# A two-layer hybrid step on one core: the first modulation, the first norm and the filter network in another order

## Chip, cores and metric

One core of one Trainium2 chip runs the whole program. The metric is the device time of one execution in microseconds (us); of several runs the median counts. The engines are TensorE (PE in the rows; PEld is its weight load), VectorE (DVE), ScalarE (ACT), GpSimd (POOL) and SyncE (SP, which issues the loads).

## The reference

Two layers process 128 context tokens and 256 latent tokens of width 1024 with the same weights, each group with its own condition vector. Of each layer the change touches the opening only:

```
mod = silu(cond) @ w_mod + b_mod
sh1, sc1, g1, sh2, sc2, g2 = split(mod, 6)
h = rms_norm(x, norm1) * (1 + sc1) + sh1
proj = h @ w_in
kf = hyena_filters(L, w1, b1, w2, b2, w3, freq)
```

`proj` feeds grouped-query attention, multi-head latent attention and a Hyena long convolution, whose spectra `kf` come out of a small filter network (two sine layers, taps with a window, an L1 norm, a Fourier transform) that does not depend on x. Branches, output projection and a ConvFFN follow.

## The kernel before

The 384 tokens stand side by side as columns, channels on the partitions: x is `xa`, 8 tiles of 128 x 384. Matmuls against weights are made of three products of a high and a low part (`mm3`, L269 to L271); `hi_lo` makes the parts (a ScalarE copy, L231, and a VectorE subtraction, L235) for weights that `load_w` (L249) brings in pieces of 1 MB through a ring of two buffers.

The first stage has four strands:

- **Modulation vectors** (`mod_load`, `mod_vec`): a vector of 1024 numbers for both conditions takes four loads of 1 MB (L329) and matmuls of 32 x 512 outputs (L338; one load is 4 instructions, 8 rows of the trace). ScalarE copies the result (L231), TensorE transposes it (L302), and VectorE adds it up with the bias (L238, 128x16) and, for vector 1, forms the scale factors `avs` (L241, 128x16). Vectors 0 and 1, shift and scale, are wanted by the first norm. Their eight loads go to `early` buffers that nothing else uses yet.
- **Squares and first norm** (`squares`, `norm_h`): ScalarE squares the x tiles (L310), VectorE sums them; TensorE adds over partitions (L382), ScalarE takes the root (L364), and TensorE spreads `rstd` over a bank (L388). Then, for each of 8 tiles, VectorE multiplies x by it (L238), ScalarE modulates the two token groups (L396, 128 and 256 columns), and the parts are made: even tiles on VectorE (cast L403, subtraction), odd ones by `hi_lo`.
- **Filter network** (`filters`): two sine layers (L428 to L436, with L460 and L464), then four jobs, for two channel halves and two orders. A job prepares weights (`prep`), makes three groups of taps (`taps`, L503, drained by a VectorE multiplication, L238; for two of them GpSimd forms a mean, L510), sums their sizes (`sizes`, L521; L538), and transforms them (`spectra`: ScalarE builds a diagonal, L546 spreads it, L558 are the transforms in three groups, each drained by VectorE, and GpSimd adds a bias at the end, L566). The filter network is a generator; each `next` issues one step.
- **First projection** (`hyena_in`): six tiles of 24 matmuls (L269 to L271) that need h and split weights.

`weave(main, (side, rate))` issues `rate` steps of a side strand for each step of `main`. Issue order is only the default: a scheduler orders each engine's instructions by priority, which follows the issue order, and by when it holds their inputs to be ready. `urgent(line, by)` issues every step of a strand at a priority raised by `by` places:

```
with tc.high_priority(offset=by):
    if next(line, line) is line:
        return
```

Within an engine the order so made is fixed, and an instruction that waits holds up all that stand behind it.

The PSUM banks are dealt out in turn, in issue order. In the first stage the filters turn through banks 0 to 3, norm and transposes through 4 to 6, modulation has 7. Once the first projection is issued (`PS_HY0`), its tiles turn through banks 1, 2 and 3, and the filters through 0 and 5. A tile that gets a bank waits until its last user is drained.

SP issues loads in its own order, with at most eight outstanding: each waits for the one eight places ahead of it.

Of the kernel before, what the change touches and what calls it, by code (L numbers as in the profile page):

```python
# [10 lines left out]
AF = mybir.ActivationFunctionType  # L11
# [30 lines left out]
SLABS = (1408, *[3072] * 9)  # L42
N_EXTRA = 3584
R_RE = 0.25
R_F0 = 3
U_CH, U_MLA = 20, 20
U_AV = 2000
FILL = (3, 2, 3)
# [137 lines left out]
def kernel(  # L186
# [8 lines left out]
    act, dve, pool, pe, sp = nc.scalar, nc.vector, nc.gpsimd, nc.tensor, nc.sync  # L195
# [83 lines left out]
    ident = ident_b.ap()  # L279
# [5 lines left out]
    cT = base.alloc(KD, 32).ap()  # L285
# [19 lines left out]
    def add_sq(k, src, first):  # L305
        if first:
            sums.append(FA.alloc(T, top=True))
        acc = sums[0].ap()
        sq = temps.get().ap()
        act.activation(out=acc if first else sq, in_=src, func=AF.Square)  # L310
        if not first:
            tt(acc, acc, sq, ALU.add)

    def squares():
        for k in range(KD):
            add_sq(k, xa[:, k], k == 0)
            yield
# [8 lines left out]
    def mod_load(l, v, k, buf):  # L326
        raw = buf.ap(2, 1024)
        src = w_mod[l, k * 256:(k + 1) * 256, v * 1024:(v + 1) * 1024]
        sp.dma_start(out=raw, in_=src.rearrange("(k p) n -> p k n", p=128))  # L329
        return raw  # L330
# [284 lines left out]
    def hyena_start(l, spec):  # L615
        y = HyenaState()
        y.l, y.spec = l, spec
        y.tok, y.late = {}, []
        line = hyena_in(y, 0, h_parts)
        next(line)  # L620
        return y, line
# [696 lines left out]
    def urgent(line, by):  # L1318

        if by < 0:  # L1320
            yield from line
            return
        while True:
# [3 lines that stand above are left out]
            yield  # L1327

    def finish(*lines):
        for g in lines:  # L1330
            for _ in g:
                pass

    def weave(main, *sides):

        credit = [0.0] * len(sides)
        for _ in main:
            for i, (g, rate) in enumerate(sides):
                credit[i] += rate
                while credit[i] >= 1:  # L1340
                    credit[i] -= 1
                    next(g, None)

    def chain(*lines):
        for g in lines:
            yield from g
# [18 lines left out]
    early = [*raw_ring.bufs, *early_parts[0].cut(2048), *early_parts[1].cut(2048)]  # L1365
    spec = new_spec()
    fl = filters(0, RA, spec, True)
    next(fl)
    sp.dma_start(out=vecs[0], in_=p_vec[0])
    sp.dma_start(out=cT, in_=p_c)  # L1370
    next(fl)
    next(fl)
    next(fl)
    ready = [mod_load(0, 0, k, early[k]) for k in range(2)]
    sp.dma_start(out=ident, in_=t_ident)
    next(fl)
    for k in (2, 3):
        ready.append(mod_load(0, 0, k, early[k]))
    for k in (0, 4):
        sp.dma_start(out=xa[:, k:k + 4], in_=p_x[:, k:k + 4])  # L1380
    for k in range(4):
        ready.append(mod_load(0, 1, k, early[4 + k]))
    act.activation(out=cT[:, :, 0:2], in_=cT[:, :, 0:2], func=AF.Silu)
    weave(chain(mod_vec(0, 0, ready[:4]), mod_vec(0, 1, ready[4:])), (fl, R_F0), (squares(), 1.2))
    for b in early_parts:
        b.free()
    parts = split_slab.whole(F32R).cut(1024)
# [2 lines left out]
    h_parts += [b.ap(KD, T) for b in h_slab.whole(F32R).cut(KD * T)]  # L1390
    hT = h_parts
    y, main = hyena_start(0, spec)
    finish(norm_h(0, 0))
    for i in range(2):
        rt = t_rope[i * 128:(i + 1) * 128]
        sp.dma_start(out=rope_a[:, i], in_=rt[:, 0:128].rearrange("p (a b) -> p a b", a=2))
# [2 lines left out]
    for l in range(NL):  # L1399
# [52 lines left out]
        if l + 1 < NL:  # L1452
            spec = new_spec()
            fl = filters(l + 1, RA, spec)
# [148 lines left out]
```

## Time and profile before

| | us |
|---|---|
| median of 3 runs | 1503.31 (1502.71 to 1505.6) |
| the profiled execution | 1507.35 |
| its span in the profile | 1505.2 |
| TensorE busy | 1460.2 (97%) |
| VectorE busy | 1005.3 (67%) |
| ScalarE busy | 750.7 (50%) |
| GpSimd busy | 97.1 (6%) |

The profiled execution is one of its own: its time is 4.0 us over the median of the runs, and its span lies 2.15 us within its time. Starts in the rows count from the beginning of the span. A row gives start, duration, engine, line, what is written and read, the count of instructions merged in it, and in brackets the idle time of the engine ahead of it with what ended that. The granted clock (PEclk) is 1.00 at 2.4 GHz and 0.50 at 1.2 GHz.

### The profile page before, as it was taken

The page shows a single profiled execution, that of the slowest core. Times are in us where ns is not written, and L with a number is a line of the kernel's source. Part 1 is how long each engine was busy: PE and PEld are TensorE (multiplying, and loading weights), DVE is VectorE, ACT ScalarE, POOL GpSimd, SP SyncE. Part 2 cuts the span into 40 slices and gives each one's busy share as a digit, 9 for nine tenths or more (in the row PEclk, how much of TensorE's full clock was granted, in tenths as well). Part 3 has the DMA queues.
Part 4 walks back from the last instruction along what each step waited for, and adds up shares of the span by engine and source line. Part 5 has one row for each costly group of instructions (what it writes and reads, how often), then busy time and mean ns, then how long its engine had stood idle before and what let it go on. Part 6 is the DMA issues. An engine that isn't in the chain of part 4 may idle for free.

```text
span 1505.2 us, 22120 instructions
## 1 busy us (share of the span) xinstructions
PE 1460.2 (97%) x8574; PEld 1342.2 (89%) x8574; DVE 1005.3 (67%) x1920; ACT 750.7 (50%) x1376; POOL 97.1 (6%) x125
## 2 busy tenths in 40 slices
PE   5799999999999999999999999999999999999997
PEld 3589889989889899999997888999888989999997
DVE  5758569547447886686775766884655777567674
ACT  4644456455444663454545444855555464344343
POOL 0222210000000000000000212100000000000000
PEclk9899999999999999999999999999999999999999
DMA  9444354434466542343266345332333533433431
GB/s 366 146 134 157 135 164 140 114 105 126 140 211 233 191 134 95 125 126 128 85 226 220 124 142 180 103 102 88 90 122 114 184 110 113 139 102 122 156 116 52
DMA packets 177496, 212.84 MB, mean 141 GB/s; under 512 B 24176, under 2 KB 160112, under 8 KB 177392
## 3 DMA queue, kind: packets, MB, share of 16 engines
q1 hardware_dynamic: 176528, 206.99, 42.6%
q0 software_dynamic: 864, 4.46, 0.9%
q8 instruction: 67, 1.10, 0.3%
q14 instruction: 37, 0.30, 0.1%
HBM read 209.29 MB, written 2.13 MB: 140 GB/s over the span
## 4 chain that ended last, share of the span: by engine, by line
PE 92%; DVE 3%; ACT 2%; DMA 1%; issue 1%; SPq 0%; DVEq 0%; ACTq 0%
PE banks L269 27%; PE banks L270 26%; PE banks L271 26%; PE banks L302 3%; PE banks L338 3%; PE banks L922 3%; DVE s L238 2%; PE banks L954 2%; PE banks L558 1%; DMA base<-in_w_in_dram 1%; DVE split L235 1%; PE banks L503 1%; ACT s L231 1%; PE banks L538 0%; DMA s<-in_p_w_dram 0%
## 5 line engine op out<-in xcount | busy, mean ns | idle before, releaser
L231 ACT ACTIVATE split<-base 128x1024 fp32r<-128x1024 f32 (+2 forms) x272 | 280.8, 1040 | 374.1 <-PE banks L270 264.1
L235 DVE TENSOR_TENSOR split<-base,split 128x1024 fp32r<-128x1024 f32 (+2 forms) x272 | 332.0, 1225 | 181.4 <-ACT split L231 180.8
L269 PE MATMUL banks<-h,split 128*128 128x384 f32 x1280 | 432.9, 342 | 5.2 <-DVE h L403 3.6
L270 PE MATMUL banks<-h,split 128*128 128x384 f32 x1280 | 435.9, 341 | 0.3
L271 PE MATMUL banks<-h,split 128*128 128x384 f32 x1280 | 433.2, 339 | 0.0
L269 PEld LDWEIGHTS banks<-h,split 128*128 128x128 f32 x1280 | 241.4, 189 | 19.5 <-issue 8.4
L270 PEld LDWEIGHTS banks<-h,split 128*128 128x128 f32 x1280 | 242.1, 189 | 4.6 <-issue 1.6
L271 PEld LDWEIGHTS banks<-h,split 128*128 128x128 f32 x1280 | 241.6, 189 | 2.4 <-issue 0.7
L270 PE MATMUL banks<-s,split 128*128 128x384 f32 x672 | 225.8, 337 | 0.0
L271 PE MATMUL banks<-s,split 128*128 128x384 f32 x672 | 225.6, 338 | 0.0
L269 PE MATMUL banks<-s,split 128*128 128x384 f32 x672 | 223.2, 339 | 1.0 <-ACT s L231 0.8
L241 DVE SCALAR_TENSOR_TENSOR s<-banks,base,s 128x127 f32<-128x127 f32 (+1 forms) x448 | 172.6, 411 | 8.4 <-ACT s L417 4.3
L231 ACT ACTIVATE s<-banks 128x384 f32<-128x384 f32 (+11 forms) x212 | 94.4, 472 | 101.3 <-PE banks L271 38.7
L231 ACT ACTIVATE s<-s 128x384 fp32r<-128x384 f32 (+3 forms) x142 | 79.0, 562 | 103.9 <-DVE s L238 57.6
L269 PEld LDWEIGHTS banks<-s,split 128*128 128x128 f32 x672 | 125.6, 188 | 4.4 <-ACT s L231 1.4
L271 PEld LDWEIGHTS banks<-s,split 128*128 128x128 f32 x672 | 126.1, 188 | 2.0 <-DVE base L241 0.8
L270 PEld LDWEIGHTS banks<-s,split 128*128 128x128 f32 x672 | 126.2, 188 | 1.4 <-issue 0.2
L238 DVE TENSOR_TENSOR s<-banks,s 128x512 f32<-128x512 f32 (+3 forms) x132 | 81.6, 645 | 43.7 <-PE banks L271 18.8
L241 DVE SCALAR_TENSOR_TENSOR base<-banks,base 128x128 f32<-128x128 f32 (+1 forms) x128 | 46.9, 412 | 74.8 <-PE banks L271 74.8
L238 DVE TENSOR_TENSOR s<-s 128x256 f32<-128x256 f32 (+4 forms) x122 | 68.0, 568 | 23.6 <-ACT s L1225 8.3
L302 PE MATMUL banks<-base,s 128*128 128x128 f32 x442 | 75.3, 274 | 2.3 <-DVE s L241 1.3
L417 ACT ACTIVATE s<-banks,base 128x384 f32<-128x384 f32 x112 | 73.2, 655 | 7.1 <-PE banks L271 7.1
(145 smaller groups left out, 1729.7 us busy)
## 6 DMA issues: line engine op xcount, KB each, us to landing
base<-in_w_in_dram SPq DMA_DIRECT2D x40, 1024.0 KB, 5.4
base<-in_ffn_up_dram SPq DMA_DIRECT2D x40, 1024.0 KB, 5.2
base<-in_w_mod_dram SPq DMA_DIRECT2D x28, 1024.0 KB, 5.2
s<-in_w_mod_dram SPq DMA_DIRECT2D x14, 1024.0 KB, 7.5
base<-in_ffn_down_dram SPq DMA_DIRECT2D x16, 896.0 KB, 5.0
base<-in_w_branch_dram SPq DMA_DIRECT2D x24, 512.0 KB, 3.5
base<-in_w_out_dram SPq DMA_DIRECT2D x8, 1024.0 KB, 5.4
base<-in_ffn_down_dram SPq DMA_DIRECT2D x8, 1024.0 KB, 5.3
```

Source lines behind the costliest of these rows:

```text
L231: act.activation(out=out, in_=in_, func=AF.Copy, scale=scale)
L235: dve.tensor_tensor(out=lo, in0=src, in1=f(hi), op=ALU.subtract)
L238: dve.tensor_tensor(out=out, in0=a, in1=b, op=op)
L241: dve.scalar_tensor_tensor(out=out, in0=a, scalar=s, in1=b, op0=op0, op1=op1)
L269: pe.matmul(out, l[0], r[0], start=start, stop=False)
L270: pe.matmul(out, l[0], r[1], start=False, stop=False)
L271: pe.matmul(out, l[1], r[0], start=False, stop=stop)
L302: pe.transpose(out, in_, ident[:n, :n])
L338: pe.matmul(gv[32 * j:32 * j + 32], cT[:, 2 * k + j // 2], raw[:, j // 2, (j % 2) * 512:(j % 2) * 512 + 512], start=k == 0, stop=k == KD / ...
L417: act.activation(out=dst, in_=src, func=AF.Identity, scale=vec(l, w1), bias=vec(l, bias))
L922: pe.matmul(out, q_of(h)[:, i * 128:(i + 1) * 128], k, start=m == 0, stop=m == len(ks) - 1)
L954: last = pe.matmul(p[b:b + 64, u], v, pT, start=start, stop=stop, tile_position=(0, b)).ins
```

## The change

The priority of five strands or parts of strands is raised by 3000 places (`U_M0`): the first three steps of the filter network (its two sine layers), both modulation vectors, the squares and the first norm. The first modulation load goes ahead of the filters' weights, the x loads and the identity are put among the modulation loads, and the second channel half's filter inputs behind the last of them. The activation of the condition vector is issued earlier. The weave issues 2.5 filter steps for each of its 12 modulation steps and not 3: 30 and not 36. No instruction is added or taken away.

```
-R_F0 = 3
+R_F0 = 2.5
+U_M0 = 3000
...
     fl = filters(0, RA, spec, True)
-    next(fl)
+    fl_now = urgent(fl, U_M0)
+    next(fl_now)
     sp.dma_start(out=vecs[0], in_=p_vec[0])
     sp.dma_start(out=cT, in_=p_c)
+    ready = [mod_load(0, 0, 0, early[0])]
+    act.activation(out=cT[:, :, 0:2], in_=cT[:, :, 0:2], func=AF.Silu)
+    next(fl_now)
+    next(fl_now)
     next(fl)
-    next(fl)
-    next(fl)
-    ready = [mod_load(0, 0, k, early[k]) for k in range(2)]
-    sp.dma_start(out=ident, in_=t_ident)
-    next(fl)
-    for k in (2, 3):
+    for k in (1, 2):
         ready.append(mod_load(0, 0, k, early[k]))
     for k in (0, 4):
         sp.dma_start(out=xa[:, k:k + 4], in_=p_x[:, k:k + 4])
+    ready.append(mod_load(0, 0, 3, early[3]))
+    sp.dma_start(out=ident, in_=t_ident)
     for k in range(4):
         ready.append(mod_load(0, 1, k, early[4 + k]))
-    act.activation(out=cT[:, :, 0:2], in_=cT[:, :, 0:2], func=AF.Silu)
-    weave(chain(mod_vec(0, 0, ready[:4]), mod_vec(0, 1, ready[4:])), (fl, R_F0), (squares(), 1.2))
+    next(fl)
+    weave(
+        urgent(chain(mod_vec(0, 0, ready[:4]), mod_vec(0, 1, ready[4:])), U_M0), (fl, R_F0), (urgent(squares(), U_M0), 1.2)
+    )
...
-    finish(norm_h(0, 0))
+    finish(urgent(norm_h(0, 0), U_M0))
```

What the scheduler makes of it is shown at three places. In the changed kernel every line from L45 on has a number that is higher by one, and by a few more behind the changed lines.

SP, the loads of the first stage from the fourth on, before (`p_w` is w3 and `p_win` the window, for one channel half each; `base`, `split` and `h` are the buffers of the modulation loads):

```order
L451 DMA s_1_138<-in_p_w_dram 128x1024
L453 DMA s_1_138<-in_p_win_dram 128x1280
L476 DMA s_1_141<-in_t_kdft_dram 128x1280
L329 DMA base_101<-in_w_mod_dram 128x2x1024 x2
L1375 DMA base_101<-in_t_ident_dram 128x128
L451 DMA s_1_141<-in_p_w_dram 128x1024
L453 DMA s_1_147<-in_p_win_dram 128x1280
L329 DMA split_108<-in_w_mod_dram 128x2x1024 x2
L1380 DMA base_101<-in_p_x_dram 128x1536 x2
L329 DMA split_108<-in_w_mod_dram 128x2x1024 x2
L329 DMA h_109<-in_w_mod_dram 128x2x1024 x2
```

and with the change:

```order
L330 DMA base_101<-in_w_mod_dram 128x2x1024
L452 DMA s_1_140<-in_p_w_dram 128x1024
L454 DMA s_1_140<-in_p_win_dram 128x1280
L477 DMA s_1_143<-in_t_kdft_dram 128x1280
L330 DMA base_101<-in_w_mod_dram 128x2x1024
L330 DMA split_108<-in_w_mod_dram 128x2x1024
L1381 DMA base_101<-in_p_x_dram 128x1536 x2
L330 DMA split_108<-in_w_mod_dram 128x2x1024
L1383 DMA base_101<-in_t_ident_dram 128x128
L330 DMA split_108<-in_w_mod_dram 128x2x1024 x2
L330 DMA h_109<-in_w_mod_dram 128x2x1024 x2
L452 DMA s_1_143<-in_p_w_dram 128x1024
```

The second w3 and window loads have moved from ahead of six modulation loads to behind the last, and x ahead of five of them.

TensorE, the last instructions ahead of the first projection matmul and that one, before:

```order
L338 MATMUL banks<-h_109,base_101 32x512 x4
L546 MATMUL banks<-s_1_141,base_101 128x512
L302 MATMUL banks<-base_101 128x128 x4
L388 MATMUL banks<-s_1_141,base_101 128x384
L503 MATMUL banks<-s_1_135 128x512 x6
L538 MATMUL banks<-base_101,s_1_211 128x1 x6
L558 MATMUL banks<-s_1_141 128x256
L558 MATMUL banks<-s_1_147,s_1_141 128x256
L558 MATMUL banks<-s_1_141 128x256
L558 MATMUL banks<-s_1_147,s_1_141 128x256
L269 MATMUL banks<-h_364,split_363 128x384 x3
```

and with the change:

```order
L339 MATMUL banks<-h_109,base_101 32x512 x8
L303 MATMUL banks<-base_101 128x128 x4
L547 MATMUL banks<-s_1_214,base_101 128x512
L559 MATMUL banks<-s_1_156,s_1_143 128x256
L559 MATMUL banks<-s_1_214,s_1_143 128x256
L559 MATMUL banks<-s_1_156,s_1_143 128x256
L559 MATMUL banks<-s_1_214,s_1_143 128x256
L504 MATMUL banks<-s_1_137 128x512 x6
L539 MATMUL banks<-base_101,s_1_156 128x1 x6
L270 MATMUL banks<-h_337,split_336 128x384
```

The norm's spread (L388, now L389) has gone ahead of the second vector's last loads, and less of the filters stands ahead of the projection. Instructions of the filters ahead of the first projection matmul, in TensorE's order as compiled:

| | taps L503 | spectra L558 | sums L538 | spreads L546 |
|---|---|---|---|---|
| before | 24 | 24 | 18 | 2 |
| with the change | 18 | 14 | 12 | 1 |

Further on, the first matmul of the attention's scores (L922) stands at place 1070 of TensorE's order before and 1133 with the change; the first that reads the attention's result stands at 1488 in both. From place 1860 on the two orders differ only in single neighbours.

VectorE, from the second vector's first addition (`base`, 128x16) to the first h tile's cast, before:

```order
L238 TENSOR_TENSOR base_101<-banks,base_101 128x16
L238 TENSOR_TENSOR s_1_107<-base_101,banks 128x384 x2
L235 TENSOR_TENSOR split_363<-base_101,split_363 128x1024
L238 TENSOR_TENSOR s_1_107<-base_101,banks 128x384 x2
L238 TENSOR_TENSOR s_1_141<-banks,s_1_147 128x512
L235 TENSOR_TENSOR split_363<-base_101,split_363 128x1024
L238 TENSOR_TENSOR s_1_211<-banks,s_1_147 128x512
L238 TENSOR_TENSOR base_101<-base_101,banks 128x16
L238 TENSOR_TENSOR s_1_147<-banks,s_1_147 128x512
L540 TENSOR_SCALAR s_1_147<-banks,base_101 128x4
L241 SCALAR_TENSOR_TENSOR base_101<-base_101 128x16
```

and with the change, from the third operation on a product of x and rstd behind the scale factors to the first drain of the third filter job's taps (ahead of these rows stand, behind the scale factors, the cast of the first h tile, two filter subtractions of 256 columns and the first h tile's low part):

```order
L239 TENSOR_TENSOR s_1_107<-base_101,banks 128x384
L404 CAST h_337<-s_1_107 128x384
L239 TENSOR_TENSOR s_1_107<-base_101,banks 128x384 x3
L239 TENSOR_TENSOR h_337<-s_1_107,h_337 128x384
L236 TENSOR_TENSOR split_336<-base_101,split_336 128x1024 x2
L239 TENSOR_TENSOR s_1_110<-banks,s_1_214 128x512 x3
L236 TENSOR_TENSOR h_337<-s_1_107,h_337 128x384
L239 TENSOR_TENSOR s_1_137<-s_1_214,s_1_137 64x512
L236 TENSOR_TENSOR h_337<-s_1_107,h_337 128x384
L236 TENSOR_TENSOR split_336<-base_101,split_336 128x1024 x2
L404 CAST h_337<-s_1_107 128x384
L239 TENSOR_TENSOR s_1_143<-banks,s_1_156 128x512
```

The vector's additions and factors now stand together with one subtraction between them, and the splits of the projection's weights, the drains of the first job's spectra and the first taps of the third job come behind them. GpSimd's addition of the first job (L566, now L567) is released by the third of the `x3` drains.

## Rows read from the trace of the kernel before

**Rows 1.** Windows: us, then PE, PEld, DVE, ACT, POOL busy, PEclk, DMA, GB/s.

```profile
300.00:400.00 100.00, 98.22 (x604) 86.72 (x603) 51.65 (x119) 51.84 (x105) 0.45 (x3) 1.00 0.42 121
```

**Rows 2.** Timeline of TensorE, 49 to 70 us.

```profile
49.75 1.06 PE L338 MATMUL banks<-h,base 128*32 128x512 f32 x8
...
52.24 0.66 PE L302 MATMUL banks<-base 128*128 128x128 f32 x4 [0.37 <-ACT base L231]
...
54.40 1.33 PE L503 MATMUL banks<-s 128*128 128x512 f32 x4 [0.36 <-DVE s L238]
55.59 1.50 PE L538 MATMUL banks<-base,s 128*128 128x1 f32 x12
62.64 1.22 PE L558 MATMUL banks<-s 128*128 128x256 f32 x2 [5.54 <-DVE s L540]
...
65.85 1.52 PE L269 MATMUL banks<-h,split 128*128 128x384 f32 x3
...
69.07 1.06 PE L338 MATMUL banks<-base 128*32 128x512 f32 x8
```

**Rows 3.** Windows of one us, columns as in rows 1.

```profile
58.00:59.00 1.00, 0.00 (x0) 0.00 (x0) 1.00 (x3) 0.00 (x0) 0.00 (x0) 0.79 0.41 131
...
68.00:69.00 1.00, 1.00 (x5) 0.79 (x3) 0.01 (x1) 1.00 (x3) 0.00 (x0) 0.59 0.00 0
69.00:70.00 1.00, 1.00 (x9) 0.16 (x8) 0.56 (x1) 1.00 (x4) 0.00 (x0) 1.00 0.06 16
```

**Rows 4.** Timeline of VectorE, 59 to 66 us.

```profile
59.96 1.21 DVE L235 TENSOR_TENSOR split<-base,split 128x1024 fp32r<-128x1024 f32 x1
61.09 0.68 DVE L238 TENSOR_TENSOR s<-banks,s 128x512 f32<-128x512 f32 x1
61.70 0.15 DVE L238 TENSOR_TENSOR base<-base,banks 128x16 f32<-128x16 f32 x1
...
62.50 0.16 DVE L241 SCALAR_TENSOR_TENSOR base<-base 128x16 f32<-128x16 f32 x1
...
64.50 0.36 DVE L403 CAST h<-s 128x384 fp32r<-128x384 f32 x1 [0.45 <-ACT s L396]
...
65.24 0.55 DVE L238 TENSOR_TENSOR h<-s,h 128x384 fp32r<-128x384 f32 x1
65.71 0.55 DVE L238 TENSOR_TENSOR s<-base,banks 128x384 f32<-128x384 f32 x1
```

**Rows 5.** Loads, 0 to 70 us: GB/s by 1.75 us; issues (KB, us to landing); SP's timeline.

```profile
GB/s 0 261 136 318 390 408 407 426 408 411 407 410 415 428 405 413 405 410 410 410 407 330 345 352 338 126 14 0 5 0 0 92 378 129 0 73 337 190 0 9
...
h<-in_w_mod_dram SPq DMA_DIRECT2D x2, 1024.0 KB, 18.6
...
18.22 3.96 SPq L329 DMA_DIRECT2D h<-in_w_mod_dram  x2
```

**Rows 6.** Timeline of ScalarE, 51 to 67 us.

```profile
51.62 0.57 ACT L231 ACTIVATE base<-banks 128x512 f32<-128x512 f32 x1
...
63.50 3.60 ACT L396 ACTIVATE s<-s,base 128x128 f32<-128x128 f32 x8
```

**Rows 7.** Timelines of GpSimd and VectorE, 55 to 59 us.

```profile
55.62 1.81 POOL L566 TENSOR_TENSOR s<-s,s 128x768 f32<-128x768 f32 x1 [9.05 <-DVE base L238]
...
56.47 2.04 DVE L235 TENSOR_TENSOR split<-base,split 128x1024 fp32r<-128x1024 f32 x1
```

**Rows 8.** Chain of waits, 67 to 103 us: start, us, what.

```profile
67.38 0.32 PE banks L270
...
84.71 1.23 PE banks L538 x12
...
98.51 0.18 PE banks L270
...
99.55 2.59 PE banks L558 x12
```

**Rows 9.** Line 922 (attention scores), to 420 us: ns min/median/max, first and last start.

```profile
L922 PE MATMUL banks<-s,s x92: 221/334/488, 245.5 to 415.7; 128*128 128x384 f32 x60, 128*128 128x128 f32 x32
```

## Prediction

> **What bounds the kernel now.** I read three views. The windows view comes first: in a stretch such as 300 to 400 us TensorE is busy 98.22 of 100 us and VectorE 51.65 [rows 1]. From about 70 us to the end the kernel is therefore a queue of TensorE work, and a change in the order of the first stage is worth what it takes out of TensorE's idle or slow time ahead of that queue, less nothing and plus nothing: work moved out of the idle time has to be done later.
>
> The timeline of TensorE shows that time [rows 2]. After the filter sums at 55.59 it stands idle for 5.54 us until 62.64, runs filter matmuls, and starts the first projection matmul at 65.85. In the windows of one us the granted clock falls inside 58 to 59 (0.79) and is back inside 68 to 69 (0.59), 1.00 at 69 [rows 3]; 0.50 is the 1.2 GHz level. So the 9 projection matmuls ahead of 69.07 (3 in the row of 65.85 and 6 behind it [rows 2]) ran at 0.32 us each and not at 0.18 [rows 8]. Had they run at the full clock, they would have had to start at 69.07 - 9 x 0.18 = 67.5. I call 67.5 the **effective start** of the queue.
>
> The timeline of VectorE shows why it starts so late [rows 4]. The last load of the second modulation vector is multiplied at 49.75 [rows 2], but VectorE adds it only at 61.70 and forms the norm's scale factors at 62.50; between, it splits weights and drains filter banks. The first h tile is cast at 64.50.
>
> **Part 1, the loads.** The last modulation load is issued from 18.22 on and takes 18.6 us [rows 5], so it lands at about 37.6. The queue moves some 410 GB/s at that time [rows 5], and serves loads in the order of issue. The new order takes one w3 and one window load (512 and 640 KB, 1.18 MB) from ahead of it: 2.9 us, so it lands at 34.7. The x loads come some 6 us earlier by the same count, and the first norm's squares, sums and square root with them; they finish near 33 and nothing waits for them, since the scale factors need the second vector. What SP now issues later (second filter half, rope tables) lands near 37, ahead of its users. The first projection weight lands near 40, before ScalarE is free for it at 42.3 below.
>
> **Part 2, the modulation vector.** From 34.7: 1.06 us of matmuls and 0.66 of transposes on TensorE [rows 2], 0.57 of copy on ScalarE [rows 6], together 37.0. VectorE then adds, does one filter subtraction that stands between the two adds and waits for a ScalarE copy queued behind the vector's own, and forms the factors: I put that at 38.5, against 62.66 before. This is what the change buys, 24 us on this value.
>
> **Part 3, from there to the first projection matmul.** ScalarE's eight modulating activations take 3.60 [rows 6]; the four narrow ones come first, so the first h tile is complete after about 2.2, at 40.8. From here VectorE is the only engine that matters, and works through the list shown with the change. The first projection tile needs bank 1. With 30 steps of the filter network issued instead of 36, that bank holds the first tap group of the third filter job, and its drain is the last row of that list. So I count to there: 8 operations of 384 columns at 0.47 (start to start), 3 casts at 0.36, 4 splits of 1024 columns at 1.13, 4 drains at 0.61 [rows 4], and three of other sizes for which I take 0.5, between the casts and the 384-column ones. That is 3.76 + 1.08 + 4.52 + 2.44 + 1.5 = 13.3 us.
>
> Into this list falls one GpSimd addition, which is released by the third drain. In the trace GpSimd ran it from 55.62 to 57.43, and the VectorE split that began at 56.47 took 2.04 and ended 1.08 after GpSimd did, where the same split alone takes 1.21 [rows 4, 7]. VectorE thus stood still until GpSimd was done. In the new list the operations behind the drain are splits and subtractions too, so I charge nearly the whole 1.81: 1.7 us. The Trainium skill (SBUF — State Buffer, Who interferes with whom) states the same for a VectorE instruction with two SBUF inputs: the second to come is blocked for the whole of the other. It speaks against this change, since it puts that piece on the critical list, and by it the charge is up to 1.8; by the loss of this one row alone (2.04 - 1.21) it would be 0.8.
>
> Sum: 40.8 + 13.3 + 1.7 = **55.8** for the first projection matmul, 10 us earlier than 65.85.
>
> **Part 4, the work that is left.** By the counts given with the change, 24 tap, 24 spectrum, 18 sum and 2 spread matmuls of the filters stood ahead of the first projection matmul, and now 18, 14, 12 and 1. What is pushed behind it costs full price in the queue: 6 taps at 0.33 [rows 2]; 10 spectrum matmuls of two passes, 20 x 0.216 = 4.3; 6 sums of two passes, 12 x 0.103 = 1.2 [rows 8]; the spread matmul has twice the columns of a spectrum pass, 0.86. Together 2.0 + 4.3 + 1.2 + 0.9 = **8.4 us** (7.7 if a tap falls to the cost of its 512 columns, about 0.23). The other moved matmuls (modulation, transposes, norm) stand ahead of it in both.
>
> **Part 5, the clock at the new start.** At the full clock the gain is 67.5 - 55.8 - 8.4 = **3.3 us**. But TensorE has pauses here too. After the spread matmul (done at 39) it waits until VectorE has taken the last product with rstd out of bank 5, which I put at 44.6; then it has some 8 us of filter work at the low level, and pauses again for about 3 us before 55.8. In the old trace the level fell 1.7 us into a pause of 5.5 and came back 6.2 us after work resumed [rows 2, 3]. If the same happens here, about 6.2 us of the queue run at half speed, 3.1 us are lost, and the gain is **0.2**. Both ends stand; I take 1.5, nearer to the low one, because the pause is longer than the 1.7 us after which the level fell. The Trainium skill (TensorE: Matmul & The Clock Gate, Part 1) says that the number of slow matmuls after a pause varies from run to run of one kernel; no row here shows that.
>
> The profiled execution took 1507.35 us, span 1505.2, and lies 4.0 over the median of 1503.31. The parts above are differences within it, and I carry the difference to the median: 1503.3 - 1.5 = **1501.8 us**. A measurement of this kernel can tell about 0.2% or 3 us from no change, so this forecast is "same".
>
> **The rivals.**
>
> *Faster, chance 0.34.* TensorE is at the full clock at the new start, and VectorE reaches the drain without the GpSimd collision: 3.3 + 1.7 = 5.0, 1498.3 us. For it: ScalarE and the loads have slack ahead of VectorE all along the list, and TensorE has more work shortly ahead of the start (8 us) than before. Against it: the list is VectorE's alone, and every wait in it adds. It counts as faster from a gain of 3.0.
>
> *Slower, chance 0.13.* The filter work that is pushed behind the start delays the Hyena chain and what follows it. By the places given with the change, the first score matmul of the attention now stands at 1133 and not 1070, while the matmuls that read the attention's result (first at 1488) have not moved; 63 places at about 0.18 are 11 us less time for the softmax. Before, those matmuls ran from 245.5 on [rows 9], and 1.78 us of 300 to 400 were idle [rows 1]. If its slack is 5 us and not 11, TensorE waits 6 us there, and 1501.8 + 6 gives 1508 us. It decides from 4.5 us of new waiting on. Against it: VectorE and ScalarE are each about half busy in that stretch (51.65 and 51.84 of 100).
>
> *No effect, within the forecast.* The raised steps could merely displace others, with VectorE equally late. The order speaks against it: fewer VectorE operations stand ahead of the first h tile.
>
> **How the numbers follow.** Forecast (within 0.2%, 1500.3 to 1506.3): 0.53. Faster 0.34, slower 0.13. The range goes from the faster rival with another 1.3 us for an earlier VectorE (1497.0) to 1505.0, which leaves out most of the slower rival. The forecast's own part of it is 1500.0 (full clock) to 1503.1 (6.2 us low), and a us or two more for VectorE's list.
>
> **What would show it.** Right: last modulation load near 34.7; scale factors near 38.5; first projection matmul near 56, released by VectorE's drain of a filter bank; granted clock 0.5 for some us from there; spectrum matmuls among the projections until about 120 us; no new TensorE waits at 240 to 340. Wrong: a start before 53 or after 59, a clock of 1.00 through the start, or TensorE idle after 70 us where it was not.

## Result and profile after

The changed kernel takes **1517.76 us** (median of 4 runs, 1515.96 to 1518.83) against 1504.05 (1502.71 to 1505.6) of the kernel before, measured beside it: ratio 1.0084, 95% interval 1.0072 to 1.0097. It is 13 us slower; the forecast was 1501.8 and its range ended at 1505.0. The profiled execution took 1517.78 us, with a span 10.7 us longer than before's 1505.2. (The profiled execution of before, 1507.35, lies 3.3 us over this median, so the two traces show 10.7 of the 13.7 us.) The page, first lines and the row of the projections (busy, mean ns, idle time ahead and what ended it):

```profile
span 1515.9 us, 22111 instructions
...
PE 1466.9 (97%) x8574; PEld 1346.7 (89%) x8574; DVE 1005.4 (66%) x1920; ACT 752.3 (50%) x1376; POOL 97.4 (6%) x125
...
L270 PE MATMUL banks<-h,split 128*128 128x384 f32 x1280 | 433.8, 342 | 11.1 <-DVE s L239 5.4
```

All of it has come about by 463 us. ScalarE's first square of the second norm, before and then changed, comes 10.6 us later, and from there to the end the distance stays about that (10.7 by the spans):

```profile
463.11 0.51 ACT L310 ACTIVATE s<-base 128x384 f32<-128x384 f32 x1
```

```profile
473.75 0.51 ACT L311 ACTIVATE s<-base 128x384 f32<-128x384 f32 x1
```

Ahead of that, two places differ: the first stage, and a stretch near 320 us. The timeline of TensorE in the first stage:

```profile
32.00 1.65 PE L389 MATMUL banks<-s,base 128*128 128x384 f32 x2 [0.92 <-DVE s L386]
33.58 1.78 PE L339 MATMUL banks<-split,base 128*32 128x512 f32 x8
35.29 1.13 PE L559 MATMUL banks<-s,s 128*128 128x256 f32 x4
36.35 1.06 PE L339 MATMUL banks<-split,base 128*32 128x512 f32 x8
37.23 1.90 PE L339 MATMUL banks<-h,base 128*32 128x512 f32 x16
39.85 0.66 PE L303 MATMUL banks<-base 128*128 128x128 f32 x4 [0.72 <-ACT base L232]
...
48.56 3.75 PE L559 MATMUL banks<-s,s 128*128 128x256 f32 x8 [3.61 <-DVE s L239]
...
60.38 0.69 PE L270 MATMUL banks<-h,split 128*128 128x384 f32 x1 [5.45 <-DVE s L239]
```

The second vector's last matmuls end at 39.1 (before: 50.8 [rows 2]). The first projection matmul starts at 60.38 and is released by VectorE's drain of a filter bank, as forecast, 5.5 us before the old start of 65.85 and 4.6 after the forecast one. The timeline of VectorE, with what it does ahead of that:

```profile
40.82 0.69 DVE L239 TENSOR_TENSOR s<-s,s 64x512 fp32r<-64x512 f32 x1
...
41.74 0.17 DVE L242 SCALAR_TENSOR_TENSOR base<-base 128x16 f32<-128x16 f32 x1
44.88 0.36 DVE L404 CAST h<-s 128x384 fp32r<-128x384 f32 x1 [2.96 <-ACT s L397]
...
53.54 2.18 DVE L239 TENSOR_TENSOR s<-s,s 64x512 fp32r<-64x512 f32 x1
...
58.77 0.69 DVE L239 TENSOR_TENSOR s<-banks,s 128x512 f32<-128x512 f32 x1
59.37 0.35 DVE L404 CAST h<-s 128x384 fp32r<-128x384 f32 x1
59.63 1.28 DVE L239 TENSOR_TENSOR s<-banks,s 128x512 f32<-128x512 f32 x2
```

The factors of the norm come at 41.74 (62.50 before [rows 4]) and the first h tile is cast at 44.88 (64.50 before): 20 us earlier, yet the projections start only 5.5 us earlier. The two rows of 64x512 are the subtraction that finishes a filter job's weights (`prep`); these are the third and the fourth job. In the kernel before the third job's ran at 21.74:

```profile
21.74 0.69 DVE L238 TENSOR_TENSOR s<-s,s 64x512 fp32r<-64x512 f32 x1
```

TensorE's windows of 1 us at the start and of 10 us near 320 us (us, TensorE busy, granted clock, DMA share, GB/s):

```profile
64.00:65.00 1.00, 1.00 (x4) 0.50 0.00 0
65.00:66.00 1.00, 1.00 (x5) 0.60 0.00 0
66.00:67.00 1.00, 1.00 (x8) 1.00 0.00 0
...
310.00:320.00 10.00, 8.08 (x60) 1.00 0.05 13
320.00:330.00 10.00, 7.74 (x37) 0.83 0.32 105
...
300.00:350.00 50.00, 44.66 (x281) 0.97 0.28 80
```

The last window in the kernel before:

```profile
300.00:350.00 50.00, 48.22 (x310) 1.00 0.47 131
```

The timeline of TensorE there, changed and then before:

```profile
321.80 0.44 PE L303 MATMUL banks<-base,s 128*128 128x128 f32 x2 [0.16 <-DVE s L236]
323.95 0.44 PE L270 MATMUL banks<-s,s 128*128 128x384 f32 x1 [1.71 <-DVE s L236]
```

```profile
316.02 0.45 PE L269 MATMUL banks<-s,s 128*128 128x384 f32 x1 [1.13 <-DVE s L235]
```

The row of 323.95 is the first matmul that reads the attention's result (place 1488 of the order). In the kernel before it started at 316.02, and of 300 to 350 us 1.78 were idle; now 5.34 are, and the clock falls (0.83 in 320 to 330). Counted in windows of one us, idle time and time lost at the low clock come to 7.0 us in this stretch, where before had 1.8: **5.2 of the 10.7 us** are lost here. Counted the same way, 4.6 us are lost in the first stage: from 0 to 70 us TensorE is idle for 23.9 us (23.3 before) and loses 7.1 at the low clock (3.1 before). What is left of these 70 us is its work, reckoned at the full clock: **39.0 us, and 43.6 before**. The work that was not done there comes later: by the groups of instructions from 70 us on, the filters' taps, sums and spectrum matmuls take 6.3 us more than before (2.1, 1.5 and 2.7). The last 0.9 us are not located.

### The profile page after: what moved, and what is told of

It is laid out like the page before. It is cut to its first block, busy times and chain, and to the rows that moved or that the text cites. A ratio compares the mean times of both kernels' runs of the same rounds, so it can differ in the third digit from the quotient of the medians.

```text
span 1515.9 us, 22111 instructions
## 1 busy us (share of the span) xinstructions
PE 1466.9 (97%) x8574; PEld 1346.7 (89%) x8574; DVE 1005.4 (66%) x1920; ACT 752.3 (50%) x1376; POOL 97.4 (6%) x125
## 4 chain that ended last, share of the span: by engine, by line
PE 92%; DMA 3%; DVE 2%; ACT 1%; SPq 1%; issue 1%; DVEq 0%; ACTq 0%
PE banks L270 27%; PE banks L271 26%; PE banks L272 26%; PE banks L303 3%; PE banks L339 3%; PE banks L923 3%; PE banks L955 2%; DMA split<-in_w_mod_dram 1%; PE banks L559 1%; DVE s L239 1%; DMA base<-in_w_in_dram 1%; SPq L1401 1%; PE banks L539 0%; DMA base<-in_t_rope_dram 0%; PE banks L504 0%
## 5 line engine op out<-in xcount | busy, mean ns | idle before, releaser
L236 DVE TENSOR_TENSOR s<-s,s 128x384 fp32r<-128x384 f32 (+2 forms) x102 | 64.8, 640 | 21.9 <-ACT s L232 16.8
```

Source lines behind the costliest of these rows:

```text
L236: dve.tensor_tensor(out=lo, in0=src, in1=f(hi), op=ALU.subtract)
```

## Experiments

Two notions come back. The **place** of the first score matmul is its number in TensorE's compiled order (1070 before, 1133 changed, as in the slower rival). **prep 3** is the start on VectorE of the 64x512 subtraction of the third filter job, which needs the w3 load of the second channel half (21.74 before, 40.82 changed). us are medians; ratios are to the kernel before on the same chip, with 95% intervals.

**e1 to e4: the rate, the priorities, the banks.** Theory A was that the lower filter rate causes the loss, theory B that the priorities do; e4 is about the bank that the first projection waits for.

```diff
 e1, in the changed kernel      -R_F0 = 2.5   +R_F0 = 3
 e2, in the changed kernel      -U_M0 = 3000  +U_M0 = -1
 e3, in the kernel before       -R_F0 = 3     +R_F0 = 2.5
 e4, in the changed kernel
-PS_HY0 = {"mm": "123", "tr": "46", "fl": "05"}
+PS_HY0 = {"mm": "623", "tr": "41", "fl": "05"}
```

> The change with its filter rate back at 3 (36 filter steps in the first weave, not 30); loads and raised priorities stay. Theory A (the rate is the cause: fewer filter steps issued early leave more of the filters behind the first projection and put its first tile behind a filter drain): 1500 to 1508 us, no idle of TensorE of more than 2 us between 300 and 350. Theory B (the raised priorities are the cause: they push filter work back and crowd VectorE's list): 1513 us or more.

> The change with no priority raised; loads in the new order and rate 2.5 stay. Theory A (rate): 1514 to 1520 us, as the changed kernel; first projection matmul at 58 to 62 us. Theory B (priorities): within 4 us of the kernel before (1500 to 1508).

> The kernel before with the rate 2.5 alone. Theory A (rate): 1510 us or more, with most of the changed kernel's loss of 13 us; Theory B (priorities), or a theory by which the loads' order is what costs: within 4 us of the kernel before.

> The changed kernel with other banks for the first projection: its tiles turn through 6, 2, 3 and the transposes through 4 and 1, so that the first tile's bank holds no filter taps. If the drain of bank 1 is what the first projection waits for (released at 59.4 us in the changed kernel): it starts at 50 to 53 us, when the splits of its weights are there, and the time is 1508 to 1514 us, since the idle time of 5.3 us between 300 and 350 stays. Rival (VectorE's list is the limit in any case, the low parts of the odd h tiles come out of it at 53.5 and 56.3): it starts early but stands still after a few matmuls, and the time is within 3 us of the changed kernel.

| | us | ratio |
|---|---|---|
| e1 | 1508.46 | 1.0018 (1.0009 to 1.0028) |
| e2 | 1521.20 | 1.0094 (1.0072 to 1.0117) |
| e3 | 1508.22 | 1.0019 (1.0010 to 1.0028) |
| e4 | 1518.18 | 1.0082 (1.0067 to 1.0098) |

A fits e1, and e2 within 1.2 us, but e3 fells it: the rate by itself costs 3 us, not 13. (e3 starts its first projection at 56.68, 9 us earlier than the kernel before, and is slower all the same.) B falls with e2. In e4 the first projection matmul starts at 46.78, and nothing is gained: TensorE then waits for h casts and drains instead, so VectorE and not the bank is the limit. What was left in common to the slow ones (e2, e4, the change) and not to e3 is the new order of the loads; e1 has that order too, at 3 filter steps, and loses 3 us.

**e5 to e8: the stall at the attention.** Theory C: a late place of the first scores makes the stall, and the stall makes most of the loss. Theory D: it takes up slack only.

```diff
 e5, in the changed kernel      -R_CH = 0.8   +R_CH = 1.5
 e6, in the kernel before       -R_CH = 0.8   +R_CH = 0.5
 e7, as e5, and                 -U_M0 = 3000  +U_M0 = -1
 e8, in the changed kernel      -R_F0 = 2.5   +R_F0 = 3.5
```

> The changed kernel with one number altered: the Hyena chain of layer 0 is woven in at 1.5 steps and not 0.8 per step of the projections (R_CH). Nothing ahead of the first projection moves; the first score matmul of the attention goes from place 1133 to 1066 of TensorE's order (1070 before the change), its reader stays. Theory C (the larger half of the loss is a stall of TensorE at the first matmuls that read the attention's result, caused by the late place of the scores): the 5.3 us idle in 300 to 350 us fall under 2, that reader starts 5 to 7 us earlier than 323.95, and the time falls by 5 to 8 to 1509 to 1513 us. Theory D (the loss is the first stage's, the late start and the filter work that is pushed behind it; the stall only takes up slack): the idle time goes elsewhere and the time stays at 1515 to 1519.

> The kernel before with one number altered: R_CH 0.5 in place of 0.8, so that the first score matmul stands at place 1165 and not 1070, with its reader where it was, and with nothing changed ahead of 70 us. Theory C: a stall appears where there was none: 5 us or more of idle time in 300 to 350 us (1.78 before), and 1510 to 1516 us in all. Theory D: no more than 2 us of it reach the end, 1502 to 1507 us.

> The changed kernel without the raised priorities (e2, 1521.2 us, score matmul at 1171) and with R_CH 1.5, which puts the score matmul at 1066. Theory C: e2's stalls in 200 to 250 and 300 to 350 us (2.6 and 5.9 us idle) fall under 3 together, and the time falls by 9 to 13 us to 1508 to 1512. Theory D: 1517 us or more.

> The changed kernel with the filters at 3.5 steps and not 2.5 in the first stage (R_F0): first projection matmul at place 124 of TensorE's order (92 changed, 115 before), first score matmul at 1068. Theory C: no stall at the attention (under 2 us idle in 300 to 350), and what is left is the first stage: a start near that of the kernel before, 64 to 68 us, and 1502 to 1507 us. Theory D: the start is what counts; with more filter work ahead of it than e1 (1508.46) it is later still, and the time lies at 1509 to 1513.

| | us | ratio |
|---|---|---|
| e5 | 1523.82 | 1.0118 (1.0103 to 1.0133) |
| e6 | 1540.34 | 1.0231 (1.0211 to 1.0250) |
| e7 | 1520.20 | 1.0098 (1.0083 to 1.0113) |
| e8 | 1510.80 | 1.0036 (1.0026 to 1.0047) |

The windows of TensorE of e5, then of e6:

```profile
150.00:200.00 50.00, 44.06 (x239) 0.94 0.45 145
300.00:350.00 50.00, 50.00 (x333) 1.00 0.43 120
```

```profile
200.00:250.00 50.00, 44.49 (x269) 0.93 0.50 155
300.00:350.00 50.00, 44.50 (x281) 0.93 0.39 110
```

The place makes the stall in both directions: at 1066 (e5) not a tenth of a us of 300 to 350 is idle, and at 1165 (e6) 5.5 are, with nothing changed ahead of 70 us. But both times miss: the faster Hyena chain of e5 brings a new stall of 5.9 us at 150 to 200 (3.7 of it waits for modulation loads), the slower one of e6 another at 200 to 250. Moving this rate trades one stall for another, and e7 repeats e5. So it is shown that the place makes this stall, and not shown that the time comes back when the stall goes; by their times e7 and e8 fall to theory D. e8 has C's undisturbed attention (48.22 busy of 50) and yet 1510.80: its first projection matmul starts at 71.13, behind more filter work than before.

Over all kernels of this study the stall goes by the place, whatever moved it, with e4 (45.4 at 1155) a little out of line (TensorE's busy time of 300 to 350 us):

| place | kernels | busy of 50 |
|---|---|---|
| 1066 | e5, e7 | 50.0 |
| 1068 to 1070 | before, e8, e9, e10, e11, e15, e16 | 48.1 to 48.4 |
| 1110 | e1, e3, e13, e17 | 46.9 to 47.4 |
| 1118 | e12, e14 | 47.0 to 47.1 |
| 1133 | changed | 44.7 |
| 1155 to 1171 | e4, e6, e2 | 44.1 to 45.4 |

What moved the place in the order is the Hyena branch: 48 matmuls of its output stand ahead of the first scores in the changed kernel (84 in e2, 27 in e1 and e3), and none before.

**e9 to e12: the loads, the priorities, and both.**

e9 is the kernel before with the new loads alone (the changed kernel with `R_F0 = 3` and `U_M0 = -1`). e10 is the kernel before with the raised priorities alone, e11 the same with `R_F0 = 2.5`: the whole change but for the order of the loads. (The activation of the condition vector goes with the loads in all three; e16 below keeps it early and is none the worse.) e12 moves the x loads of the changed kernel:

```diff
-    for k in (0, 4):
-        sp.dma_start(out=xa[:, k:k + 4], in_=p_x[:, k:k + 4])
     ready.append(mod_load(0, 0, 3, early[3]))
     sp.dma_start(out=ident, in_=t_ident)
     for k in range(4):
         ready.append(mod_load(0, 1, k, early[4 + k]))
+    for k in (0, 4):
+        sp.dma_start(out=xa[:, k:k + 4], in_=p_x[:, k:k + 4])
```

> The kernel before with the new order of loads alone (filters at 3 steps, no raised priority). First projection matmul at place 119 (115 before), first score matmul at 1070, as before. Theory C (what the change loses behind 70 us goes by the place of the first score matmul): idle time of 300 to 350 us stays at 1.8, and the time is that of before within 2 us, 1503 to 1507. Theory F (the new order of loads is itself the cause, whatever the rate): 1510 or more. e1, which has the priorities too and the place 1110, was 1508.46.

> The kernel before with the raised priorities alone (old loads, filters at 3 steps). First projection matmul at place 119, first score matmul at 1070. Theory C: no new stall at 300 to 350 us; the loads end no earlier, so the second vector is ready 3 us later than in the changed kernel; 1502 to 1507 us. A rival, theory G (the priorities push VectorE's drains of the filters back and so cost by themselves, e1 over before): 1508 to 1511.

> The changed kernel with the old order of loads (rate 2.5 and raised priorities stay). First projection matmul at place 103 (92 changed), first score matmul at 1070 (1133 changed). Theory C: the stall at 300 to 350 us goes back from 5.3 to 1.8 us idle and with it most of the loss: 1502 to 1508 us. Theory G: the priorities and the rate lose it in the first stage, whatever the place: 1512 to 1518.

> The changed kernel with the x loads behind all modulation loads. The norm's spread matmul (L389) then stands behind the second vector's matmuls in TensorE's order, where in the changed kernel it stands ahead of the last three loads' and waits until 32.00. First score matmul at 1118 (1133 changed). If that waiting matmul and the slow clock behind it are what made the second vector late (last modulation matmuls to 39.1 and the factors at 41.7 in place of the 38.5 forecast): the last modulation matmuls end before 37 and the first h tile is modulated from 40 or earlier, unless the norm's root is late instead. If TensorE was not the cause: the last modulation matmuls end at 38.5 or later. Theory C: at place 1118 between e1's 2.6 and the changed kernel's 5.3 us idle in 300 to 350 us, 1508 to 1515 us in all.

| | us | ratio |
|---|---|---|
| e9 | 1513.07 | 1.0048 (1.0033 to 1.0063) |
| e10 | 1502.64 | 0.9980 (0.9970 to 0.9989) |
| e11 | 1503.44 | 0.9982 (0.9973 to 0.9992) |
| e12 | 1514.61 | 1.0057 (1.0042 to 1.0072) |

The order of the loads is the cause (theory F in e9, C against G in e11), and without it the change beats the kernel before by 0.2%. Eight of the kernels (before and the change among them) have every combination of loads, rate and priorities. With the other two held equal, the new loads cost 7 us (e9 over before), 11 (e2 over e3), 6 (e1 over e10) and 15 (the change over e11). The rate of 2.5 costs 7 and 10 us with the new loads (e2 over e9, the change over e1), and 3 and 0.3 with the old ones (e3 over before, e11 over e10). So the loss of the change takes both: loads that come late and few filter steps issued beside them.

VectorE and TensorE of e11:

```profile
21.25 0.69 DVE L239 TENSOR_TENSOR s<-s,s 64x512 fp32r<-64x512 f32 x1
...
40.12 2.32 DVE L239 TENSOR_TENSOR s<-s,s 64x512 fp32r<-64x512 f32 x1
...
55.45 0.35 DVE L404 CAST h<-s 128x384 fp32r<-128x384 f32 x1
```

```profile
60.18 1.31 PE L270 MATMUL banks<-h,split 128*128 128x384 f32 x3
```

This comparison bears the conclusion. In e11 the first h tile is cast at 55.45, **10.6 us later** than in the changed kernel, and the first projection matmul starts at 60.18, 0.2 us earlier. An early h is worth nothing while VectorE still has the filters' work to do. The window of 30 to 50 us, VectorE (us, busy, granted clock, DMA share, GB/s), e11 and then the changed kernel:

```profile
30.00:50.00 20.00, 16.83 (x37) 0.91 0.75 266
```

```profile
30.00:50.00 20.00, 11.84 (x33) 0.71 0.74 258
```

VectorE works 5.0 us less in the changed kernel while the loads come in (the kernel before: 14.62, so 2.8 less), TensorE 4.8 less, and at a lower clock. TensorE in the same window, before, e11 and changed:

```profile
30.00:50.00 20.00, 17.57 (x102) 1.00 0.76 270
```

```profile
30.00:50.00 20.00, 17.14 (x95) 0.91 0.75 266
```

```profile
30.00:50.00 20.00, 12.38 (x58) 0.71 0.74 258
```

That work is found again behind 44.88.

e9 loses elsewhere than the change, at 70 to 100 us (3.4 us idle and 3.0 at the low clock, in windows of one us), so theory C is too narrow: the place is one way to lose, and not the only one. G falls with e10.

e12 tells of the prediction's second part. With the norm's spread matmul out of the way the second vector's last matmuls end at 34.4 and not at 39.1, and the factors are there at 36.31 and not at 41.74:

```profile
32.49 1.92 PE L339 MATMUL banks<-h,base 128*32 128x512 f32 x16
```

Not all of the 5.4 us is TensorE's: the modulation loads also stand ahead of 1.5 MB of x here, and the last of them lands at 31.5 and not at 34.6. The norm then is late (the root at 45.04), and the time is 4 us under that of the change by the ratios.

**e13 to e17: which load.** Theory H: the loads of the filters' second half, without which the third filter job can't begin. Theory I: the others. Then J: the early x loads, and K: the first modulation load ahead of the filters' first half.

```diff
 e13, in the changed kernel (e15: the same with R_F0 = 3)
     next(fl_now)
     next(fl)
+    next(fl)
     for k in (1, 2):
...
-    next(fl)
     weave(
 e14, in e11
     sp.dma_start(out=ident, in_=t_ident)
-    next(fl)
     for k in (2, 3):
...
+    next(fl)
     weave(
 e16, in e13
-    for k in (0, 4):
-        sp.dma_start(out=xa[:, k:k + 4], in_=p_x[:, k:k + 4])
     ready.append(mod_load(0, 0, 3, early[3]))
     sp.dma_start(out=ident, in_=t_ident)
+    for k in (0, 4):
+        sp.dma_start(out=xa[:, k:k + 4], in_=p_x[:, k:k + 4])
 e17, in e13
-    ready = [mod_load(0, 0, 0, early[0])]
     act.activation(out=cT[:, :, 0:2], in_=cT[:, :, 0:2], func=AF.Silu)
...
     next(fl)
+    ready = [mod_load(0, 0, 0, early[0])]
     for k in (1, 2):
```

> The changed kernel with one thing put back: the loads of the filters' second half (w3 and window) are issued ahead of the other modulation and x loads, as before, and not behind the last modulation load. Theory H (these two loads are the cause: without them the third filter job's weights are prepared by VectorE at 40.82 and not at 21.74, so VectorE and TensorE run out of filter work from 30 to 50 us and the work left stands on the way to the first projection): the third job's weights are prepared near 21, the first projection matmul starts at 57 to 60, and the time is near e11's: 1501 to 1508 us. Theory I (the other moved loads are the cause: modulation, x and identity): 1513 us or more.

> e11 (old loads, raised priorities, filters at 2.5 steps; 1503.44 us) with one thing moved: the loads of the filters' second half go behind the last modulation load. First score matmul at place 1118 (1070 in e11). Theory H: the third job's weights are prepared at 38 us or later, VectorE is idle for 7 us or more of 30 to 50 us (3.2 in e11), and the time rises by 8 to 15 us to 1511 to 1518. Theory I: 1502 to 1507 us.

> e13 with the filters at 3 steps, as in the kernel before; first projection matmul at place 119, first score matmul at 1070. Theory H: no loss is left of the load order; e10, which differs from it by the order of modulation, x and identity loads alone, took 1502.64 us, so 1501 to 1506 us. Theory I: like e1, 1508 us or more.

> e13 with the x loads behind the fourth modulation load and the identity load, as in the kernel before (the first modulation load stays ahead of the filters' first half). First score matmul at place 1070 (1110 in e13). Theory J (the early x loads are the rest: the norm's instructions come between the filters' and the first scores get a later place): idle time of 300 to 350 us back from 3.1 to 1.7, and 1502 to 1506 us. Theory K (the first modulation load, which holds back the filters' first half, is the rest): 1508 to 1511 us.

> e13 with the first modulation load behind the filters' loads, as in the kernel before (the x loads stay early). First score matmul at place 1110, as in e13. Theory K: 1502 to 1506 us. Theory J: 1508 to 1511 us, with 3 us idle at 300 to 350 us.

| | us | ratio | prep 3 |
|---|---|---|---|
| e13 | 1510.17 | 1.0037 (1.0022 to 1.0052) | 17.18 |
| e14 | 1512.03 | 1.0049 (1.0033 to 1.0064) | 40.65 |
| e15 | 1505.63 | 1.0004 (0.9994 to 1.0014) | 17.11 |
| e16 | 1503.09 | 0.9989 (0.9979 to 0.9998) | 16.98 |
| e17 | 1509.43 | 1.0028 (1.0016 to 1.0039) | 15.62 |

SP's timeline, the loads of the second half, in e11 and in e14:

```profile
5.76 0.44 SPq L452 DMA_DIRECT2D s<-in_p_w_dram  x1
6.25 0.45 SPq L454 DMA_DIRECT2D s<-in_p_win_dram  x1
```

```profile
19.01 3.48 SPq L452 DMA_DIRECT2D s<-in_p_w_dram  x1
22.53 1.21 SPq L454 DMA_DIRECT2D s<-in_p_win_dram  x1
```

VectorE in e14, to be set against e11's 21.25:

```profile
40.65 0.69 DVE L239 TENSOR_TENSOR s<-s,s 64x512 fp32r<-64x512 f32 x1 [0.20 <-ACT s L232]
```

H holds for the larger part. These two loads alone cost 10 us when moved late in e11 (0.9982 to 1.0049) and give 7 back when moved early in the changed kernel (1.0084 to 1.0037), both of 1505. The traces say the same: the square of 463.11 starts at 465.58 in e13, 8.2 us earlier than in the changed kernel, and at 467.88 in e14, 7.6 later than in e11 (460.31); and TensorE's work of 0 to 70 us, reckoned at the full clock, is 39.0 in the changed kernel and 44.1 in e13, 43.2 in e11 and 39.1 in e14. At 3 filter steps the same two loads cost only some 2 us (1.0018 in e1, 1.0004 in e15, with intervals that overlap). In e14 VectorE's busy time of 30 to 50 us fell only from 16.83 to 15.74 and not by the 4 expected; it is TensorE's that fell (17.14 to 12.70), since the third job's taps were not there. But e13 took 1510.17 and not the 1508 or less that H expected, and e15, though within H's range, is still 3.6 us over e10 (0.9980). The rest goes with the early x loads: e16 gains another 7 us on e13 (1.0037 to 0.9989), and e17, whose interval overlaps e13's, shows nothing for K. TensorE's windows of e13, then e16:

```profile
300.00:350.00 50.00, 46.93 (x283) 0.97 0.40 117
```

```profile
300.00:350.00 50.00, 48.21 (x310) 1.00 0.46 137
```

The first scores are at 1110 in e13 and 1070 in e16. Idle time and clock explain 3.0 us of the difference (in windows of one us 4.8 lost against 1.8). The spans are 5.4 apart. At the square of 463.11 (465.58 in e13, 462.09 in e16) the difference is 3.5; of the rest, 1.8 are idle time at 800 to 850 us (4.0 in e13, 2.2 in e16), in a part that neither kernel changes, and stay unexplained. In the first 70 us e16 does even less of TensorE's work than e13 (40.9 against 44.1), and where it wins that back is not located. So that the early x loads cost is shown by e16; J's mechanism accounts for 3.0 us of it. e13 is also a case of an early start that wins nothing: 56.26, as forecast for the change, and 1510 us.

e10, e11 and e16 are the versions that beat both kernels. Their intervals overlap; none is shown to be the best.

## Why the prediction was wrong

**Part 1** had the time right and the cost wrong; this is the step that failed. The last modulation load, issued at 17.83, lands 16.8 us later, at 34.6, against the 34.7 forecast. (In the kernel before it landed at 39.0 and not at 37.6, so the gain was 4.4 us and not 2.9.) But the sentence "What SP now issues later (second filter half, rope tables) lands near 37, ahead of its users" priced the move at nothing. It looked at the users where the new order puts them. In the kernel before, the user, prep 3, ran at 21.74; it moved back to 40.82 with its w3 load, which landed at 18.2 before and lands at 35.9 now. In the time from 30 to 50 us, which that load had filled with filter work, TensorE was busy for 12.38 us and not 17.57. Measured: 7 to 10 us (e13, e14). The early x loads, which the same part also had at nothing ("nothing waits for them"), cost another 7 (e16).

**Part 2** came 3.2 us late (41.74 for 38.5). The load was there at 34.6, so TensorE was the limit: the spread matmul L389 waited for its operand until 32.00, the clock fell, and behind it four loads' matmuls and one of the filters ran without a gap to 39.1. e12, without that wait (and with earlier loads), has the factors at 36.31. It cost little in the end, since e11 starts its projections as early with factors at 52.30.

**Part 3** was right in its sum: from the first cast (44.88) to the first projection matmul (60.38) it took 15.5 us, 15.0 forecast. The GpSimd collision is in it as priced: GpSimd added from 53.12 to 55.17, and VectorE's subtraction of 53.54 took 2.18 and not the 0.69 of 40.82, 1.5 us more (1.7 forecast). The Trainium skill (SBUF — State Buffer, Who interferes with whom) has the rule, and the trace agrees: the subtraction ended at 55.72, 0.55 after GpSimd. What I missed is why the list was there: some 5.5 us of it are filter work (the operations of 512 and 256 columns), of which e11 does more ahead of h.

**Parts 4 and 5.** The effective start, the start plus what the low clock cost behind it, is 60.38 + 2.7 = 63.1 (65.85 + 1.5 = 67.3 before): 4.2 us gained. Part 4 held: by the groups, the filter matmuls behind the start take 9.1 us more than before (38.9 against 29.8; 8.4 forecast). That leaves a loss of 4.9, near the 4.6 counted in the first 70 us, where I forecast a gain of 1.5. The clock came out near the low end, at 0.50 until 65 and 1.00 from 66 on, but by luck: the pause was 5.5 us long and not 3, and the level held for the first 4.0 us of it (0.98 in 58 to 59), longer than the forecast pause. So the first stage alone turned the sign: it started 4.6 us later than forecast, and the sum had no term for the work that the loads held back.

**The slower rival** had this part of the mechanism and nearly its price: 6 us of waiting forecast, 5.2 measured, by the place that it named, of which 3.5 are waiting and 1.7 the low clock behind it. It had nothing for the first stage, and e5 and e7 show that the time need not come back when this stall goes. Its chance of 0.13 was too small. The argument against it, VectorE and ScalarE half busy in that stretch, says nothing about a chain of dependent steps that starts late.

**The faster rival** falls with both its conditions: the clock was not full at the start, and VectorE met GpSimd's addition. That e10 and e11 are 3 us faster is not its doing: e11 starts at the low clock too, and TensorE's work of the first 70 us is 43.2 in both and 43.6 before, so idle time and clock of the first stage do not explain their gain, which stays open. **No effect** falls too.

## What to carry to other kernels

Ask of a load that is moved back where its user stood in the kernel before, not where the new order has put it: the user moves with the load, and the time it filled stays empty. Try such a move at more than one setting of what runs beside it: the same two loads cost some 2 us at 3 filter steps and 7 to 10 at 2.5. An operand that comes 20 us earlier is worth only what the engine that must take it is free to do with it; count that engine's whole list up to the event, in idle time before as well as after. And where a schedule is made by a tool, look for the first instructions of the next long chain of dependencies in its order: a shift of 60 places there went with 5 us of waiting and slow clock at 320 us, far from the edit.

## What was not expected of the hardware

The granted clock fell after less idle time than in the first stage of the kernel before. TensorE had been busy to 31.08, waited 0.92 us, and ran L389 and the following at half speed (windows of one us, TensorE):

```profile
30.00:31.00 1.00, 1.00 (x11) 1.00 1.02 406
31.00:32.00 1.00, 0.08 (x2) 0.83 1.02 406
32.00:33.00 1.00, 1.00 (x2) 0.50 1.01 406
...
34.00:35.00 1.00, 1.00 (x8) 0.50 1.07 426
35.00:36.00 1.00, 1.00 (x7) 0.96 1.05 417
```

Ahead of it stood 16 rows of matmuls of one column (L383, L539) and four of transposes. L389 took 1.65 us, and 0.91 in e14, where it ran at 36.05 between modulation matmuls. In the kernel before the level fell 1.5 us into a pause (57.1 to 58.6 by [rows 2, 3]; the prediction's 1.7 is a little too long), and here, ahead of the first projection matmul, only 4.0 us into one, behind as many rows of taps and sums. It came back inside 35 to 36, and after the start at 60.38 inside 65 to 66: neither is a constant to be put into a sum.
